# Block 1 of a fused two-matmul kernel with one plain h pair in place of three, and three w1 form stores placed behind the x transposes

## The chip, the cores and the metric

The kernel runs on one core of one Trainium2 chip. The metric is the device time of one execution in microseconds (us), given as the median of several runs. All times inside an execution come from a hardware profile of one run, counted from the start of its span.

## The reference

```python
y = np.matmul(x, w1) + b1                          # x (16, 512, 768), w1 (768, 3072)
y = 0.5 * y * (1.0 + erf(y / np.sqrt(2.0)))        # GELU
return np.matmul(y, w2).astype(np.float32)         # w2 (3072, 768)
```

There are 8192 rows of x. Inputs and output are float32; the kernel computes in bf16 with float32 sums.

## The kernel before

**Row blocks.** The 8192 rows are cut into ten blocks of 768 rows and a last one of 512 (`pairs`; "block p" below is the p-th of them). Each block is computed in two stages: first the hidden layer, whose GELU values go to the tile `g`, then the product with w2, whose sums go through PSUM to the tile `ot` and from there to the output.

**First stage.** The 24 chunks of 128 hidden columns are taken as 12 "h pairs" j = (j, j + 12). There are two ways to compute one h pair for a block.
- Plain: `plain` (matmuls at L396) does 6 matmuls for each of the two columns and each half of the rows, 24 matmuls of 128x384 in all, straight from the bf16 copy of w1.
- Formed: a Winograd scheme of 7 products, P1 to P7 (`product1`, matmuls at L154), 3 matmuls each, 21 in all. It needs 7 "forms" of the w1 pair (sums and differences, made once by `make_w1`: one copy on ScalarE, four sums on VectorE, the halves of which are called `one` and `two`) and four sums of x (`sum_x`, tile `xft`). ScalarE copies P1's bank (`ps<-ps`, L102) before P2 can add to the copy.

In block 0 all pairs are plain. In block 1 the pairs 0, 1 and 2 are plain and nine are formed. In all later blocks twelve are formed. The loop over formed pairs runs in steps: step s works on the pair `js[s]`, and `fill(s)` puts one piece of other work (a half of a form or a sum for the second stage) behind P2 and one behind P6.

**Where forms live.** A set of forms is made in a staging area that is free just then: parts of `ot` (called otf), of `st` (stf), of `ev`, of `xft`. The tuple `order1` says which pair is formed n-th and `stage` where. From the staging area it is stored to DRAM (`w1f`). The stores of n = 0 to 3 are held in the list `waiting`; those of n = 4 and 5 go on SyncE's queue, later ones on GpSimd's. The forms come back from `w1f` through a ring of five slots, which take the place of the raw w1 in `w1t`; a slot can be filled once every raw pair under it has been formed (and, if plain, used): `free_slots`, `fill_slot`. In block 1 the pairs 9 and 10 are read directly from their staging areas instead (`where`).

**Second stage.** A block's rows form two groups, G0 and G1, of three row tiles. A group takes 15 products M0 to M14 (`rest`, `part2`, 8 matmuls each at L229) in the order M14, M8, M4, M7, M6, M13, M12, M2, M1, M5, M3, M10, M9, M11, M0. Most of them read a sum of `g` blocks that VectorE makes (`gsum`: M2a, M2b and so on) in slots of `st`; G1's M2, M12 and M10 have the slots 4, 5 and 6. `finish2` takes each product out of its PSUM bank, with copies on ScalarE and adds on VectorE into `ot`. Several products share a bank: M11 adds to the bank of M10, and M0 to that of M9, so that M0's matmuls need VectorE's add of M9 to be done.

**What sets the order.** Every instruction is kept in program order on its engine, and each queue of DMAs too. Around the end of block 0's first stage SyncE's queue holds two w1 form stores (n = 0 from `ot`, n = 1 from `st` slots 4 to 6), then six transposes (L287) that bring block 1's x into `xt`, then the stores of n = 2 and 3. The loads of x for these transposes are on GpSimd's queue behind all loads of w1 and w2; the fifth and sixth of them reuse the buffers of the first two and so wait for the first two transposes.

Of the kernel before, what the change touches and what calls it, by code (L numbers as in the profile page):

```python
# [12 lines left out]
P = 128  # L13
# [20 lines left out]
def kernel(  # L34
# [21 lines left out]
    QH = QC // 2  # L56
    SLOT = 7 * KH * P
    RING = 5
    PLAIN = 3
    GRP = 3 * KC * P  # L60
    FIRST = -(-2 * GRP // SLOT)
    HOME = (0, None, 2 * GRP, 4 * GRP)
    pairs = []
    r = 0
# [46 lines left out]
    def sub(dst, a, b):  # L111
        inorder(nc.vector.tensor_tensor(out=dst, in0=a, in1=b, op=ALU.subtract))  # L112

    seq = [3, 9, 10, 4, 5, 6, 7, 8, 11] + [j for _ in pairs[2:] for j in range(HP)]
    where = {}

    def fill_slot(k):
# [8 lines left out]
    formed = set()  # L126

    def index(p, j):
        return seq.index(j) if p == 1 else (p - 1) * HP - PLAIN + j

    def place_h(hc):
        h, j = divmod(hc, HP)
# [87 lines left out]
    def gsums(G, *ms):  # L220
        return [lambda m=m: gsum(G, m) for m in ms]
# [8 lines left out]
                out=ps[:, :NB], lhsT=lhs[:, c, :], rhs=w2t[:, c, WF[m], :],  # L230
                start=(m in OPENS and c == 0), stop=(c == QC - 1), skip_group_check=True))

    spare = 1
    turn = {2: 3, 1: 0, 3: 2}

    def store(t, r, last, c0=0, c1=N):
        dma(nc.sync if last else nc.gpsimd, out=of[r:r + P, c0:c1], in_=t[:, c0:c1])
# [100 lines left out]
    def raw(j):  # L338
# [1 line left out]
        return w1_pair(j // 3).rearrange("p (b kc c) -> p b kc c", b=4, kc=KH)[:, :, :, c0:c0 + P]  # L340

    made = 0
    stage = ((otf, 0), (stf, 4 * QC * P), (evf, 0), (xftf, 0), (evf, 0), (xftf, 0),
             (otf, N * 4), (stf, 4 * QC * P), (otf, 0), (stf, QC * P), (stf, 4 * QC * P), (stf, QC * P))
    order1 = (3, 4, 5, 6, 7, 8, 9, 11, 10, 0, 1, 2)
    waiting = []

    def make_w1():
        nonlocal made
        n = made  # L350
        made += 1
        j = order1[n]
        a = raw(j)
        area, o = stage[n]
        s = area[:, o:o + SLOT].rearrange("p (f kc c) -> p f kc c", f=7, kc=KH)
        copy("act", s[:, 0:2], a[:, 1:3])

        def one():
            add(s[:, 2], a[:, 1], a[:, 2])
            add(s[:, 3:5], a[:, 0:4:2], a[:, 1:4:2])  # L360

        def two():
            sub(s[:, 5], a[:, 2], a[:, 0])
            sub(s[:, 6], a[:, 1], a[:, 3])
            if n < 4:
                waiting.append(lambda queue: dma(queue, out=w1f[j], in_=area[:, o:o + SLOT]))
            else:
                dma(nc.sync if n < 6 else nc.gpsimd, out=w1f[j], in_=area[:, o:o + SLOT])
            formed.add(j)
            if j in (9, 10):  # L370
                where[seq.index(j)] = area[:, o:o + SLOT]

        return one, two

    ready = [(k + FIRST) % RING for k in range(RING)]

    def free_slots(plain_done=0):
        while ready:
            k = ready[0]
            need = {j for j in range(HP) if HOME[j // 3] is not None  # L380
                    and HOME[j // 3] < (k + 1) * SLOT and HOME[j // 3] + 2 * GRP > k * SLOT}
            if not need <= formed or any(plain_done <= j < PLAIN for j in need):
                break
            fill_slot(ready.pop(0))

    def form_w1(plain_done=0):
        for f in make_w1():
            f()
        free_slots(plain_done)

    def plain(hc, half):
        py = bank()
# [138 lines left out]
    make_w2(7)  # L531
    for m in ("M1", "M3b", "M10a", "M10b", "M11a", "M11b"):
        gsum(blk[0], m)
    for f in waiting[:2]:
        f(nc.sync)


    ts = [[dict() for _ in range(HP)] for _ in pairs]

    def ahead(p):  # L540
        j = PLAIN if p == 1 else 0
        for m in ("P1", "P7"):
            product1(ts[p][j], m, p, j, pairs[p][1])

    def run(fs):
        for f in fs:
            f()
# [13 lines left out]
    for p, (r0, w) in enumerate(pairs):  # L561
# [3 lines left out]
        full = len(G1["tiles"]) == 3  # L565

        if p > 0:
            js = seq[:HP - PLAIN] if p == 1 else list(range(HP))
            last = len(js) - 1
            more = []  # L570
            if p == 1:
                hcs = [hc for j in range(PLAIN) for hc in (j, HP + j)]
                for n, hc in enumerate(hcs):
                    if n in (0, 1, 3):
                        form_w1()
                    if n in (1, 2):
                        sum_x(2 * n - 2, w)
                        sum_x(2 * n - 1, w)
                    plain(hc, 0)
                    if n == len(hcs) - 1:  # L580
                        ahead(p)
                    plain(hc, 1)
                free_slots(PLAIN)
                more = [0, 1, 3]

            both = (G0, G1) if full else (G0,)
            todo = [(js.index(QH - 1) if QH - 1 in js else 0, f) for G in both for f in gsums(G, *EARLY)]
            todo += [(js.index(2 * QH - 1), f) for G in both for f in gsums(G, *MIDDLE)]
            if p == 1:
                todo[2:4] = [(3, f) for _, f in todo[2:4]]  # L590

            halves = []

            def fill(s):
                if s in more and not halves:
                    more.remove(s)
                    halves.extend(make_w1())
                    halves.append(None)
                if halves and halves[0] is None:
                    halves.clear()  # L600
                elif halves:
                    halves.pop(0)()
                    if len(halves) == 1:
                        halves.clear()
                        free_slots(PLAIN)
                    return
                if s <= last and todo and s > todo[0][0] + (p > 1 or todo[0][0] > 0):
                    todo.pop(0)[1]()

            def step1(s, m):  # L610
                if 0 <= s <= last:
                    product1(ts[p][js[s]], m, p, js[s], w)

            for s in range(last + 1):
                if s == 0:
                    order = ((0, "P2"), (0, "P4"), (-1, "P1"), (0, "P6"))
                elif s == 1:
                    order = ((0, "P7"), (1, "P5"), (0, "P2"), (1, "P3"), (0, "P4"), (0, "P6"))
                else:
                    order = ((0, "P1"), (0, "P7"), (1, "P5"), (0, "P2"), (1, "P3"), (0, "P4"), (0, "P6"))  # L620
                for d, m in order:
                    step1(s - d, m)
                    if m in ("P2", "P6"):
                        fill(s)
            step1(last, "P5")
            part2(G0, "M14", range(0, 5))
            step1(last, "P3")
            part2(G0, "M14", range(5, QC))
            finish2(G0, "M14")
            if nxt is not None:  # L630
                prepare_x(*nxt, otf[:, 2 * G1["o"][2] * K:])
            rest(G0, "M8")
            rest(G0, "M4")
            run([f for _, f in todo] + gsums(G0, *LATE))
            rest(G0, "M7")
            qs = [h * QH + q for q in range(QH) for h in range(2)]
            part2(G0, "M6", qs)
            finish2(G0, "M6")
            part2(G0, "M13", qs)
            finish2(G0, "M13")  # L640
        else:
            raws = ("M4", "M14", "M13", "M8", "M7", "M6")
            prepare_x(*nxt, xftf[:, SLOT:])
            for f in waiting[2:]:
                f(nc.sync)
            for c in range(QC - 1):
                for m in raws:
                    part2(G0, m, (c,))
            for m in raws:
                part2(G0, m, (QC - 1,))  # L650
                finish2(G0, m)
# [10 lines left out]

        if full:
            run(take(9))
            for m in ("M14", "M8", "M4"):
                rest(G1, m)
            if p > 0:
                for k in range(4):
                    sum_x(k, nxt[1])
            for m in ("M7", "M6", "M13"):  # L670
                rest(G1, m)
            if p == 0:
                form_w1()
            middle(G1, lambda n: [form_w1] if p == 0 and n == 5 else [])
            if p > 0:
                ahead(p + 1)
            rest(G1, "M0")
        else:
            a = lambda k: block(G1, 0, k)
            d12, d13 = st[:, 4, :, :], st[:, 5, :, :]  # L680
            sub(d12, a(0), a(1))
            sub(d13, a(0), a(2))
            t = ot[:, G1["o"][2], :]
            for n, terms in enumerate(((("b31", a(2)), ("M4", a(1)), ("b11", d12)),
                                       (("M13", a(2)), ("b22", a(1)), ("b12", d13)))):
                ps = bank()
                for f, lhs in terms:
                    for c in range(QC):
                        inorder(nc.tensor.matmul(  # L689
                            out=ps[:, :NB], lhsT=lhs[:, c, :], rhs=w2t[:, c, WF[f], :],  # L690
                            start=(f == terms[0][0] and c == 0), stop=(f == terms[2][0] and c == QC - 1)))
                copy("act", t[:, n * NB:(n + 1) * NB], ps[:, :NB])
                store(t, G1["rows"][0], True, n * NB, (n + 1) * NB)
# [30 lines left out]
```

## Time and profile before

| what | value |
|---|---|
| median of 3 runs | 881.35 us (881.0 to 882.9) |
| profiled execution | 881.5 us, its span 879.7 us |
| TensorE matmul busy | 872.2 us, 99% of the span |
| VectorE busy | 588.4 us, 67% |
| ScalarE busy | 399.2 us, 45% |
| granted TensorE clock | 1.0 throughout |

The profiled execution takes 1.8 us more than its span, and is 0.15 us above the median. "Busy" is the time in which an engine has an instruction under way. "PE" is TensorE's matmul unit, "DVE" VectorE, "ACT" ScalarE, "POOL" GpSimd, "SP" SyncE; a "q" behind a name is that engine's queue of issued DMAs. "Landing" is the time from a DMA's issue to its completion. Block 0's first stage ends at 57.2 us, its second at 97.6 us, and block 1's first stage at about 140 us.

### The profile page before, as it was taken

To read this page: it belongs to the slowest core of one execution; us is meant where nothing else is said; L and a number is where in the kernel's file an instruction comes from. 1 tells how busy PE (TensorE), PEld (TensorE's weight loads), DVE (VectorE), ACT (ScalarE), POOL (GpSimd) and SP (SyncE) were. 2 spreads that over 40 slices of the span, in tenths; PEclk is the share of its full clock that TensorE was granted. 3 is DMA by queue.
4 is the path that set the end of the run, shared out by engine and by line. 5 is a ranking of instruction groups with operands and counts; after the bars stand their busy time and mean duration, and the time that the engine had idled before them with its cause. 6 is when DMAs were issued, how large, how long until landed. Compare 5 with 4: busy or idle time off the path is not lost.

```text
span 879.7 us, 14114 instructions
## 1 busy us (share of the span) xinstructions
PE 872.2 (99%) x5508; PEld 533.3 (61%) x5508; DVE 588.4 (67%) x1104; ACT 399.2 (45%) x789; POOL 84.4 (10%) x153
## 2 busy tenths in 40 slices
PE   9999999999999999999999999999999999999998
PEld 6665656666666666666666666666666666666774
DVE  2889777757765766677578566756765776577654
ACT  3642384157227613741671276147316712751560
POOL 6200110010110011000101100010001011000000
PEclk9999999999999999999999999999999999999999
DMA  9996589276717734671766277356718663761621
GB/s 195 237 198 162 210 285 276 72 201 202 167 77 225 217 98 126 219 194 64 211 210 163 63 232 210 91 162 211 167 73 225 199 150 84 228 191 54 208 68 72
DMA packets 89031, 147.31 MB, mean 167 GB/s; under 512 B 50796, under 2 KB 68228, under 8 KB 88964
## 3 DMA queue, kind: packets, MB, share of 16 engines
q1 hardware_dynamic: 64832, 97.04, 36.5%
q0 software_dynamic: 24096, 49.36, 23.9%
q8 instruction: 43, 0.70, 0.3%
q14 instruction: 24, 0.20, 0.1%
q10 hardware_dynamic: 36, 0.01, 0.0%
HBM read 123.19 MB, written 33.42 MB: 178 GB/s over the span
## 4 chain that ended last, share of the span: by engine, by line
PE 89%; DMA 6%; DVE 3%; issue 1%; ACT 1%; POOL 0%; DVEq 0%; ACTq 0%; POOLq 0%
PE ps L229 45%; PE ps L154 43%; DMA w2t<-in_w_dram 5%; DVE w2t L112 1%; PE ps L689 1%; DMA w1t<-in_w_dram 1%; ACT g L143 1%; DVE ot L109 0%; DVE st L112 0%; DVE g L112 0%; DVE ps L112 0%; ACT ot L102 0%; DVE st L109 0%; DVE w2t L109 0%; POOL xft L79 0%
## 5 line engine op out<-in xcount | busy, mean ns | idle before, releaser
L154 PEld LDWEIGHTS <-w1t 128*128 128x128 bf16 x2415 | 236.1, 98 | 145.6 <-issue 1.9
L143 ACT ACTIVATE g<-ps,b1t 128x384 bf16<-128x384 f32 (+1 forms) x411 | 222.8, 571 | 78.8 <-PE ps L154 56.2
L154 PE MATMUL ps<-xft,w1t 128*128 128x384 bf16 (+1 forms) x1380 | 257.4, 320 | 0.5 <-ACT ps L102 0.5
L229 PE MATMUL ps<-w2t,g 128*128 128x384 bf16 x1512 | 257.5, 326 | 0.1
L229 PEld LDWEIGHTS <-g 128*128 128x128 bf16 x1512 | 147.9, 98 | 97.7 <-issue 0.3
L154 PE MATMUL ps<-xt,w1t 128*128 128x384 bf16 (+1 forms) x1035 | 201.1, 320 | 0.2
L109 DVE TENSOR_TENSOR ot<-ot,ps 128x384 f32<-128x384 f32 x231 | 125.4, 552 | 108.7 <-PE ps L229 53.1
L229 PE MATMUL ps<-w2t,st 128*128 128x384 bf16 x1008 | 170.8, 326 | 1.0 <-DVE st L109 1.0
L102 ACT COPY ot<-ps 128x384 f32<-128x384 f32 x128 | 60.9, 481 | 232.5 <-PE ps L229 213.9
L229 PEld LDWEIGHTS <-st 128*128 128x128 bf16 x1008 | 98.5, 98 | 66.4 <-DVE st L109 1.4
L102 ACT COPY ps<-ps 128x384 f32<-128x384 f32 (+1 forms) x117 | 53.0, 453 | 134.6 <-PE ps L154 134.6
L112 DVE TENSOR_TENSOR ev<-ps,ev 128x384 f32<-128x384 f32 (+1 forms) x117 | 63.6, 544 | 71.4 <-PE ps L154 70.5
L112 DVE TENSOR_TENSOR ps<-ps,ev 128x384 f32<-128x384 f32 (+1 forms) x117 | 64.6, 552 | 44.4 <-PE ps L154 43.8
L104 DVE COPY ev<-ps 128x384 f32<-128x384 f32 (+1 forms) x117 | 63.3, 541 | 23.1 <-PE ps L154 23.0
L143 ACT ACTIVATE g<-ev,b1t 128x384 bf16<-128x384 f32 (+1 forms) x117 | 70.9, 606 | 11.3 <-DVE ev L112 11.3
L112 DVE TENSOR_TENSOR st<-g 128x1024 bf16<-128x1024 bf16 x107 | 72.9, 682 | 0.9 <-ACT g L143 0.9
L79 POOL DMA_DIRECT2D out_dram<-ot x60 | 32.6, 544 | 343.1 <-DVE ot L109 343.1
L112 DVE TENSOR_TENSOR g<-g 128x1024 bf16<-128x1024 bf16 x84 | 57.4, 684 | 0.4
L79 POOL DMA_DIRECT2D xb<-in_x_dram x38 | 20.6, 548 | 339.7 <-DMA xt<-xb 328.7
L396 PE MATMUL ps<-xt,w1t 128*128 128x384 bf16 x252 | 41.6, 326 | 0.0
L396 PEld LDWEIGHTS <-w1t 128*128 128x128 bf16 x252 | 24.6, 98 | 16.2
L109 DVE TENSOR_TENSOR g<-g 128x1024 bf16<-128x1024 bf16 x42 | 29.0, 689 | 1.1
(70 smaller groups left out, 262.4 us busy)
## 6 DMA issues: line engine op xcount, KB each, us to landing
w1t<-w1f SPq DMA_DIRECT2D x115, 672.0 KB, 4.5
out_dram<-ot POOLq DMA_DIRECT2D x60, 384.0 KB, 2.6
xb<-in_x_dram POOLq DMA_DIRECT2D x38, 192.0 KB, 4.6
w2t<-in_w_dram POOLq DMA_DIRECT2D x8, 576.0 KB, 25.9
ot<-in_x_dram POOLq DMA_DIRECT2D x18, 192.0 KB, 7.8
w1f<-st POOLq DMA_DIRECT2D x4, 672.0 KB, 6.6
w1t<-in_w_dram POOLq DMA_DIRECT2D x4, 576.0 KB, 25.4
w1f<-ev SPq DMA_DIRECT2D x2, 672.0 KB, 3.6
```

Source lines behind the costliest of these rows:

```text
L79: inorder(queue.dma_start(out=out, in_=in_))
L102: inorder(nc.scalar.copy(out=dst, in_=src))
L104: inorder(nc.vector.tensor_copy(out=dst, in_=src))
L109: inorder(nc.vector.tensor_tensor(out=dst, in0=a, in1=b, op=ALU.add))
L112: inorder(nc.vector.tensor_tensor(out=dst, in0=a, in1=b, op=ALU.subtract))
L143: inorder(nc.scalar.activation(out=g[:, place_h(hc), half, :w], in_=src, func=ACTF.Gelu, bias=b1t[:, hc:hc + 1], scale=sign))
L154: inorder(nc.tensor.matmul(out=ps[:, :w], lhsT=forms[:, W1F[m], kc, :], rhs=moving1(m, kc, w), start=(kc == 0 and m in ("P1", "P7")), stop ...
L229: inorder(nc.tensor.matmul(out=ps[:, :NB], lhsT=lhs[:, c, :], rhs=w2t[:, c, WF[m], :], start=(m in OPENS and c == 0), stop=(c == QC - 1), ...
L396: inorder(nc.tensor.matmul(out=py[:, :HW], lhsT=lhs[:, kc, (j % 3) * P:(j % 3 + 1) * P], rhs=xt[:, kc, half, :], start=(kc == 0), stop=(kc ...
L689: inorder(nc.tensor.matmul(out=ps[:, :NB], lhsT=lhs[:, c, :], rhs=w2t[:, c, WF[f], :], start=(f == terms[0][0] and c == 0), stop=(f == ter ...
```

## The change

- Block 1 has one plain pair, 9, instead of three. Eleven pairs are formed. Pairs 6, 7 and 8 are read directly from staging areas.
- The forms are made in another order, and the first six of them before block 1: n = 4 before G1's products in block 0, n = 5 after M13 of G1. The last six are made in block 1, two beside its plain products and four in the steps 0, 2, 3 and 4.
- The four sums of x for block 1 move from beside block 1's plain products to the end of block 0, between VectorE's adds of G1's M10, M9, M11 and M0.
- Of the four held w1 form stores, the first (n = 0) is issued from ScalarE's queue after block 0's plain products; those of n = 1, 2 and 3 go to SyncE's queue behind the transposes. Before, n = 0 and 1 were issued in front of the transposes at about 30 us.
- The ring starts with slot 0. The sums for the second stage of block 1 move to later steps, as the pairs come in another order, and G0's late sums go ahead of G1's.

```diff
-    PLAIN = 3
+    PLAIN = (9,)
+    DIRECT = (6, 7, 8)
...
-    seq = [3, 9, 10, 4, 5, 6, 7, 8, 11] + [j for _ in pairs[2:] for j in range(HP)]
+    seq = [0, 6, 7, 8, 1, 2, 3, 4, 5, 10, 11] + [j for _ in pairs[2:] for j in range(HP)]
...
-    spare = 1
-    turn = {2: 3, 1: 0, 3: 2}
+    spare = 3
+    turn = {2: 1, 1: 0, 3: 2}
...
-    stage = ((otf, 0), (stf, 4 * QC * P), (evf, 0), (xftf, 0), (evf, 0), (xftf, 0),
-             (otf, N * 4), (stf, 4 * QC * P), (otf, 0), (stf, QC * P), (stf, 4 * QC * P), (stf, QC * P))
-    order1 = (3, 4, 5, 6, 7, 8, 9, 11, 10, 0, 1, 2)
+    ST1, ST4, OTB = (stf, QC * P), (stf, 4 * QC * P), (otf, N * 4)
+    stage = ((otf, 0), ST4, (evf, 0), (xftf, 0), (evf, 0), (xftf, 0), ST4, (otf, 0), OTB, ST1, ST4, (otf, 0))
+    order1 = (3, 4, 5, 0, 1, 2, 6, 7, 8, 10, 11, 9)
...
-            if j in (9, 10):
+            if j in DIRECT:
                 where[seq.index(j)] = area[:, o:o + SLOT]
...
-    ready = [(k + FIRST) % RING for k in range(RING)]
+    ready = list(range(RING))
...
-    for f in waiting[:2]:
-        f(nc.sync)
+    waiting.pop(0)(nc.scalar)
...
             if p == 1:
-                hcs = [hc for j in range(PLAIN) for hc in (j, HP + j)]
+                hcs = [hc for j in PLAIN for hc in (j, HP + j)]
                 for n, hc in enumerate(hcs):
-                    if n in (0, 1, 3):
-                        form_w1()
-                    if n in (1, 2):
-                        sum_x(2 * n - 2, w)
-                        sum_x(2 * n - 1, w)
+                    form_w1()
                     plain(hc, 0)
...
-                free_slots(PLAIN)
-                more = [0, 1, 3]
+                more = [0, 2, 3, 4]
...
-            todo = [(js.index(QH - 1) if QH - 1 in js else 0, f) for G in both for f in gsums(G, *EARLY)]
-            todo += [(js.index(2 * QH - 1), f) for G in both for f in gsums(G, *MIDDLE)]
-            if p == 1:
-                todo[2:4] = [(3, f) for _, f in todo[2:4]]
+            done = [max(n for n, j in enumerate(js) if j < k * QH) for k in (1, 2)]
+            todo = [(done[0], f) for G in both for f in gsums(G, *EARLY)]
+            todo += [(done[1], f) for G in both for f in gsums(G, *MIDDLE)]
...
-                if s <= last and todo and s > todo[0][0] + (p > 1 or todo[0][0] > 0):
+                if s <= last and todo and s > todo[0][0] + 1:
                     todo.pop(0)[1]()
...
-            run([f for _, f in todo] + gsums(G0, *LATE))
+            left = [f for _, f in todo]
+            if p == 1:
+                run(left[:-len(MIDDLE)] + gsums(G0, *LATE) + left[-len(MIDDLE):])
+            else:
+                run(left + gsums(G0, *LATE))
...
             prepare_x(*nxt, xftf[:, SLOT:])
-            for f in waiting[2:]:
+            for f in waiting:
                 f(nc.sync)
...
         if full:
             run(take(9))
+            if p == 0:
+                form_w1()
             for m in ("M14", "M8", "M4"):
                 rest(G1, m)
...
             if p == 0:
                 form_w1()
-            middle(G1, lambda n: [form_w1] if p == 0 and n == 5 else [])
+            at = {5: (0,), 6: (1,), 7: (2,)} if p == 0 else {}
+            middle(G1, lambda n: [lambda k=k: sum_x(k, nxt[1]) for k in at.get(n, ())])
             if p > 0:
                 ahead(p + 1)
             rest(G1, "M0")
+            if p == 0:
+                sum_x(3, nxt[1])
```

## The prediction

> **What bounds the kernel now.** I read the page's engine row first: TensorE is busy for 99% of the span, so only fewer matmuls or less idle TensorE can count.
>
> ```profile
> PE 872.2 (99%) x5508; PEld 533.3 (61%) x5508; DVE 588.4 (67%) x1104; ACT 399.2 (45%) x789; POOL 84.4 (10%) x153
> ...
> L396 PE MATMUL ps<-xt,w1t 128*128 128x384 bf16 x252 | 41.6, 326 | 0.0
> ```
>
> The timeline of TensorE comes next (start, duration, instructions). In long runs a 128x384 matmul starts every 0.1625 us: the 66 plain ones from 97.64 to 108.36 us are 10.72 us. Held against this pace, the rows show where TensorE starts late.
>
> ```profile
> 65.03 4.06 PE L229 MATMUL ps<-w2t,st 128*128 128x384 bf16 x24
> 70.10 1.47 PE L229 MATMUL ps<-w2t,st 128*128 128x384 bf16 x8 [1.00 <-DVE st L109]
> ...
> 72.71 2.76 PE L229 MATMUL ps<-w2t,st 128*128 128x384 bf16 x16
> 75.54 10.56 PE L229 MATMUL ps<-w2t,g 128*128 128x384 bf16 x64
> ...
> 109.34 1.14 PE L396 MATMUL ps<-xt,w1t 128*128 128x384 bf16 x6
> 110.99 0.65 PE L154 MATMUL ps<-xft,w1t 128*128 128x384 bf16 x3 [0.51 <-ACT ps L102]
> ```
>
> M5 of block 0's G0 could start at 65.03 + 24 x 0.1625 = 68.93 and starts at 70.10: 1.17 us lost. M11 could start at 72.71 + 16 x 0.1625 = 75.31 and starts at 75.54: 0.23. P2 of block 1's first formed pair could start at 109.34 + 0.975 = 110.32 and starts at 110.99: 0.67. One more of 0.19 us is at 124.41, where the row before gives 123.73 + 3 x 0.1625 = 124.22.
>
> Why M5 is late: the chain of waits is VectorE without a gap from a load of w2 that lands at 53.76 to M5's sum (69.36 in the timeline of VectorE, last fence). The loads are late because the DMA engines are full: their share is over 1.1 in every stretch of 2 us from 4 to 64 us. The DMA view, asked for single loads, gives their landings. They were issued at 13.39, 14.84, 16.31 and 39.83 us.
>
> ```profile
> w2t<-in_w_dram POOLq DMA_DIRECT2D x1, 576.0 KB, 19.8
> ...
> w1t<-in_w_dram POOLq DMA_DIRECT2D x1, 576.0 KB, 24.7
> ...
> w2t<-in_w_dram POOLq DMA_DIRECT2D x1, 576.0 KB, 26.0
> ...
> xb<-in_x_dram POOLq DMA_DIRECT2D x1, 192.0 KB, 20.5
> ```
>
> They land at 33.2, 39.5, 42.3 and 60.3. Loads of this size land 2.85 us apart elsewhere (42.3 to 59.4 in six steps), so the gap of 6.35 holds 3.5 us of other traffic: the two form stores in SyncE's timeline at 29.51 and 30.30.
>
> ```profile
> 29.51 0.33 SPq L79 DMA_DIRECT2D w1f<-ot  x1
> 30.30 0.33 SPq L79 DMA_DIRECT2D w1f<-st  x1
> 60.39 2.63 SPq L287 DMA_TRANSPOSE xt<-xb  x2
> ...
> 68.63 4.03 SPq L287 DMA_TRANSPOSE xt<-xb  x2
> 72.76 0.52 SPq L79 DMA_DIRECT2D w1f<-ev  x1
> ```
>
> **The change part by part.**
>
> Matmuls: pairs 1 and 2 (by count, two of the three plain) go from 24 to 21 matmuls each. 6 x 0.1625 = 0.98 us less. All twelve forms are made before as after, so ScalarE's and VectorE's forms, stores and gathers are only moved. The 8 GELUs of 0.57 us for two pairs stay; a formed pair adds a copy (0.45) on ScalarE and three operations (0.55 each) on VectorE, beside matmuls, as in the other formed steps.
>
> Stores n = 0 and 1 leave 30 us: every load that lands from 39.5 on comes 3.5 us sooner. VectorE's last make_w2 then ends at about 60.7 in place of 64.2, and its next six sums (3.9 us) at 64.6, before the first of block 0's products is to be added (65.0). M5's sum is then ruled by M12's add (matmuls done at 66.33): 66.5 + 0.5, and the sum to 67.7, before 68.93. The 1.17 goes, and the 0.23 too, as M10's add follows its matmuls at once: 1.40 us.
>
> Store n = 0 now stands on ScalarE's queue behind the last GELU (58.02) and in front of M4's copy (64.42). ScalarE is idle for these 6.4 us, so its issue (0.33 on SyncE's row, 0.54 on GpSimd's) is covered. M14's copy and M7's add write over its source and wait for its landing: 3.3 us (the `ev` store at 72.76) to 7.7 (the `st` store among loads), so 61.7 to 66.1. I take 63.5, as the loads end at 60 us. At 66.1 M14's copy ends at 66.5, 0.2 after M2 wants its bank, and M5's sum at 68.6, still in time. Cost 0, at worst 0.2.
>
> Store n = 1 now stands behind the transposes. It reads `st` slots 4 to 6, and G1's M2a writes slot 4. M2a therefore waits for its landing. Queued behind M2a on VectorE is M9's add, and TensorE's M0 waits for that.
>
> ```profile
> 69.36 0.68 DVE L109 TENSOR_TENSOR st<-g 128x1024 bf16<-128x1024 bf16 x1
> ...
> 75.41 0.68 DVE L112 TENSOR_TENSOR st<-g 128x1024 bf16<-128x1024 bf16 x1
> 76.01 0.54 DVE L109 TENSOR_TENSOR ot<-ot,ps 128x384 f32<-128x384 f32 x1
> ```
>
> The third row is M9's add, 0.60 behind M2a. After the change M0 is due at 68.93 + 5 x 1.30 = 75.43, so M2a must start by 75.43 - 0.05 - 0.54 - 0.60 = 74.25. The transposes: the first waits for its load (60.3, now 56.8) and for block 0's plain matmuls (57.4), so starts at 57.45, 2.9 sooner. Its landing (3.7 us) lets the fifth load go, and so on as before: SyncE is through at 72.7 - 2.9 = 69.8, n = 1 goes first and lands 3.3 us later, at 73.1. VectorE reaches M2a at 73.45. No wait; 1.1 us are to spare.
>
> n = 2 and 3 land some 2 us after n = 1 (75 to 77); the next use of `ev` is at about 81. n = 4's form (1.35 us) in front of G1's products, and n = 5's at 85.8, lie where VectorE waited 0.70 and 0.75 for ScalarE anyway. The four sums of x (0.66 each) between the adds: M10's add ends at 94.5 on the old clock, the sum at 95.2, M9's add at 95.7, M0 due at 96.34; 0.6 to spare. `xft` is free at 91.2 (n = 5's store, 87.4 + 3.8).
>
> Block 1's start: n = 8 is the first form there whose area waits for G1's last output store. Before, forms from 103.06 on waited for such a store (5.6 us landing, among fills), and ScalarE, working off that backlog, copied P1 late: the 0.67. After, the store lands in 2.6 to 5.6 us, at about 100 to 103; VectorE needs the area at 102.3, ScalarE its half, which the store before frees 1.1 sooner, at 101.7; and P1's copy stands in front of both. The 0.67 goes. The 0.19 came from a form's ScalarE copy waiting 0.60 for a store from the same `st` area, one step after it; now four steps lie between: it goes too. Steps 2, 3 and 4 each carry a form; in a step of 3.41 us ScalarE then has 2.4 (its rows from 120.09 on) + 0.74, VectorE 1.7 (three of 0.55) + 1.4: both fit.
>
> Ring: the last form (step 4) frees slots 3 and 4, and pair 4 is needed at step 7, 5.6 us after that fill can go. Before, the fill at 124.1 had the same 5.6 us (step 6 at 129.77) with the same store and x loads behind it, and landed in 4.4. No cost. The sums for `st` move to steps 8 to 10 and behind them; as many (11) as before stand between the last step and M7's add.
>
> Sum: 0.98 + 1.40 + 0.67 + 0.19 = 3.24 us. The profiled 881.5 becomes 878.3 (it was 0.15 above the median, which I leave).
>
> **The rivals.**
>
> 1. The moved store slows the transposes. n = 0 moves at 59 to 63 us beside them; if they lose what the loads lost to one store (3.5 / 2 = 1.75), n = 1 lands at 74.85, M0 0.6 late: 878.9. For it: the DMA share was over 1.1 there. Against: 3.5 us of other traffic has left the stretch. The Trainium skill, "DMA: Bandwidth & Descriptors", section "Issuing engines are not separate DMA queues", says that DMAs of ScalarE, SyncE and GpSimd run on the same 16 engines and interleave; by it the store is not free on a queue of its own. The gap of 6.35 us agrees.
>
> 2. The loads do not come sooner (another limit than bandwidth). The 1.40 stays, n = 1 lands at 72.76 + 3.3 = 76.1, M9's add ends 1.2 later, and M0 moves from 76.84 to 77.3: 881.5 - 0.98 - 0.86 + 0.46 = 880.1. Against: the gap stands exactly where the stores are.
>
> 3. Pair 4's fill is late. At the landing of the next fill before (9.0 us at 125.5) step 7 waits 3.4: 881.7, no change. For: forms in steps 3 and 4 put two stores closer to the fill. Against: 4.4 in the same place.
>
> 4. Slower: n = 1's landing. VectorE stands at M2a until then, with M9's add and M0 behind. From 77.5 on the loss eats the 3.24; from 79.2 the kernel is slower by over 0.2%. With the transposes as before and that store's own landing of before (7.7), it lands at 80.5, M0 starts at 81.7, 6.3 late: 884.5. For: it was placed behind six transposes. Against: the 3.3 of the store that stood there.
>
> 5. The change does less in block 1: ScalarE's backlog stays (0.67 and 0.19), 879.1.
>
> **How the numbers follow.** Forecast 0.50; rival 1 0.17, 2 0.08, 3 0.10, 4 0.10, 5 0.05. A difference under 0.2% (1.76 us) can't be told from none. Forecast, 1 and 5 are below 879.6: faster 0.72. 2 and 3 are within: 0.18. 4: slower 0.10. The range takes the forecast and rivals 1, 2 and 5 (0.80): from 877.5 (0.4 for the medians' spread and 0.4 for small idle times not listed) to 881.0 (880.1 with the spread of before's runs).
>
> **What would show it.** 5502 matmuls; no late start at block 0's M5, M11 and M0, nor at block 1's first P2; the first transpose at 57.5 and w2's loads 3.5 us sooner; M2a of G1 at 73.5 to 74.3. An idle TensorE at M0 with VectorE waiting for `w1f<-st` would show rivals 1, 2 or 4 by its size; an idle TensorE at the start of step 7 of block 1, waiting for `w1t<-w1f`, rival 3.

## The result and the profile after

| what | before | after |
|---|---|---|
| median, same chip (5 runs each) | 881.35 us (881.0 to 883.31) | 878.16 us (877.83 to 878.35) |
| profiled execution, its span | 881.5 us, 879.7 us | 877.96 us, 876.2 us |
| TensorE matmuls, busy | 5508, 872.2 us | 5502, 870.6 us |

The ratio is 0.9956, with a 95% interval of 0.9945 to 0.9967: faster by 3.2 us. Of the 3.5 us between the two spans, 0.19 lies ahead of everything that was changed: block 0's second stage starts at 57.04 instead of 57.23, as TensorE's first plain matmul ran that much earlier. From there to the end it is 819.16 us instead of 822.47: 3.31 us, where the prediction's sum was 3.24.

The first line is the engine row of the page after, the second the group of plain matmuls, 204 in place of 252.

```profile
PE 870.6 (99%) x5502; PEld 532.9 (61%) x5502; DVE 591.8 (68%) x1110; ACT 400.4 (46%) x791; POOL 84.4 (10%) x153
...
L396 PE MATMUL ps<-xt,w1t 128*128 128x384 bf16 x204 | 33.8, 326 | 0.0
```

The timeline of TensorE after (start, duration, instructions) answers to the rows with late starts. None of these rows has a wait any more.

```profile
64.84 5.36 PE L229 MATMUL ps<-w2t,st 128*128 128x384 bf16 x32
70.04 1.46 PE L229 MATMUL ps<-w2t,g 128*128 128x384 bf16 x8
71.34 2.76 PE L229 MATMUL ps<-w2t,st 128*128 128x384 bf16 x16
73.94 10.56 PE L229 MATMUL ps<-w2t,g 128*128 128x384 bf16 x64
...
99.94 1.14 PE L396 MATMUL ps<-xt,w1t 128*128 128x384 bf16 x6
100.92 0.65 PE L154 MATMUL ps<-xft,w1t 128*128 128x384 bf16 x3
```

The 24 matmuls ahead of M5 and M5's 8 are now one row of 32; M11 starts at 73.94 = 71.34 + 16 x 0.1625, M0 is inside the row of 64, and P2 of block 1's first formed pair starts at 100.92 = 99.94 + 0.975. The row at 124.39 follows the one at 123.90 after 3 x 0.1625. All four gaps are closed.

The same four loads in the DMA view, one by one. They were issued at 12.65, 14.11, 15.57 and 35.93 us.

```profile
w2t<-in_w_dram POOLq DMA_DIRECT2D x1, 576.0 KB, 20.1
...
w1t<-in_w_dram POOLq DMA_DIRECT2D x1, 576.0 KB, 21.5
...
w2t<-in_w_dram POOLq DMA_DIRECT2D x1, 576.0 KB, 22.9
...
xb<-in_x_dram POOLq DMA_DIRECT2D x1, 192.0 KB, 20.6
```

They land at 32.75, 35.6, 38.5 and 56.5. The gap between the first two, 6.35 us before, is 2.86, like the one behind it.

What had been left thin is seen on SyncE's queue and on VectorE:

```profile
56.61 3.62 SPq L287 DMA_TRANSPOSE xt<-xb  x2
60.34 2.81 SPq L287 DMA_TRANSPOSE xt<-xft  x2
67.00 2.78 SPq L287 DMA_TRANSPOSE xt<-xb  x2
69.97 0.43 SPq L79 DMA_DIRECT2D w1f<-st  x1
```

```profile
66.27 1.48 DVE L109 TENSOR_TENSOR ot<-ot,ps 128x384 f32<-128x384 f32 x3 [2.04 <-ACT ot L102]
67.67 0.68 DVE L109 TENSOR_TENSOR st<-g 128x1024 bf16<-128x1024 bf16 x1
...
73.72 0.68 DVE L112 TENSOR_TENSOR st<-g 128x1024 bf16<-128x1024 bf16 x1
74.32 0.54 DVE L109 TENSOR_TENSOR ot<-ot,ps 128x384 f32<-128x384 f32 x1
```

M5's sum runs from 67.67 to 68.35 and is due at 64.84 + 24 x 0.1625 = 68.74. Store n = 1 is issued at 69.97 and lands 3.3 us later, at 73.3. M2a (73.72) does not wait. M0 is due at 73.94 + 8 x 0.1625 = 75.24, so by the prediction's steps M2a must start by 75.24 - 0.05 - 0.54 - 0.60 = 74.05: the store has 0.75 us to spare, VectorE 0.3.

### The profile page after: what moved, and what is told of

Read it like the earlier page. It is cut to its first block, busy times and chain, and to the rows that moved or that the text cites. A ratio compares the mean times of both kernels' runs of the same rounds, so it can differ in the third digit from the quotient of the medians.

```text
span 876.2 us, 14116 instructions
## 1 busy us (share of the span) xinstructions
PE 870.6 (99%) x5502; PEld 532.9 (61%) x5502; DVE 591.8 (68%) x1110; ACT 400.4 (46%) x791; POOL 84.4 (10%) x153
## 4 chain that ended last, share of the span: by engine, by line
PE 98%; DVE 1%; ACT 0%; issue 0%; DVEq 0%; ACTq 0%
PE ps L229 47%; PE ps L154 44%; PE ps L396 5%; PE ps L691 1%; PE ps L459 1%; PE ps L406 1%; PE ps L421 0%; DVE ps L112 0%; DVE st L112 0%; DVE ev L112 0%; ACT g L143 0%; DVE ev L104 0%; DVE g L112 0%; DVE xt L104 0%; ACT ot L102 0%
## 5 line engine op out<-in xcount | busy, mean ns | idle before, releaser
L154 PEld LDWEIGHTS <-w1t 128*128 128x128 bf16 x2436 | 238.2, 98 | 146.1 <-issue 0.9
L396 PE MATMUL ps<-xt,w1t 128*128 128x384 bf16 x204 | 33.8, 326 | 0.0
L109 DVE TENSOR_TENSOR st<-st,g 128x1024 bf16<-128x1024 bf16 x42 | 28.9, 688 | 0.8
```

The lines of the kernel that those rows point to most:

```text
L154: inorder(nc.tensor.matmul(out=ps[:, :w], lhsT=forms[:, W1F[m], kc, :], rhs=moving1(m, kc, w), start=(kc == 0 and m in ("P1", "P7")), stop ...
L396: inorder(nc.tensor.matmul(out=py[:, :HW], lhsT=lhs[:, kc, (j % 3) * P:(j % 3 + 1) * P], rhs=xt[:, kc, half, :], start=(kc == 0), stop=(kc ...
```

## The experiments

All kernels are the changed one with one edit, but for the second, which is the kernel before with one edit. Each has its median, range and number of runs; on the chips used, the kernel before measured 882.12 us (for the first four experiments), 882.19 (the next two) and 882.22 (the last three), and the ratios are against these. To compare profiles, I use the time from the start of block 0's second stage to the end of the span: before 822.47, after 819.16.

**Stores n = 0 and 1 back at 30 us.**

```diff
-    waiting.pop(0)(nc.scalar)
+    for f in waiting[:2]:
+        f(nc.sync)
...
-            for f in waiting:
+            for f in waiting[2:]:
```

> The changed kernel with the first two form stores (n = 0 and 1) issued in front of the transposes as before; all of block 1's part is kept. Theory (the stores at 30 us delay the w2 and x loads by 3.5 us): the load after the stores lands 6.35 us after the one ahead of it, block 0's M5 is late by 1.17 us and M11 by 0.23 again, the first transpose starts near 60.4, and the span is 1.40 longer than the changed kernel's 876.2: 877.6 (time 879.4). Rival (the gain in block 0 comes from something else in the change, such as the order of forms): M5 on time, span 876.2.

Measured: 880.34 us (879.58 to 881.18, 11 runs), 0.9978 of before [0.9970, 0.9987]. From the stage's start to the end 820.98, 1.82 more than the changed kernel. TensorE's timeline:

```profile
64.92 4.06 PE L229 MATMUL ps<-w2t,st 128*128 128x384 bf16 x24
70.41 1.48 PE L229 MATMUL ps<-w2t,st 128*128 128x384 bf16 x8 [1.43 <-DVE st L109]
```

M5 was due at 68.82 and is 1.59 late, M11 0.23 late: 1.82, all of the difference, at the two places named, while block 1's gaps stay closed. The amount is above the 1.40 because the loads landed 0.29 later and the stage began 0.11 earlier than in the profile of before. The stores among the loads cause M5's late start: shown.

**The move of the stores alone, in the kernel before.**

```diff
-    for f in waiting[:2]:
-        f(nc.sync)
+    waiting.pop(0)(nc.scalar)
...
-            for f in waiting[2:]:
+            for f in waiting:
```

> The kernel before with only the move of the form stores (n = 0 on ScalarE's queue, n = 1 to 3 behind the transposes). Theory: M5 and M11 of block 0 on time, 1.40 us less, while block 1's late P2 (0.67) and the 0.19 stay: span 879.7 - 1.4 = 878.3, time 880.1. M2a of G1 starts at 73.7 and does not hold up M0. Rival (the store in front of M2a costs what it saves when the rest of the change is not there): M0 late, span 879.7 or more.

Measured: 880.38 us (880.0 to 882.34, 11 runs), 0.9984 [0.9975, 0.9992]. Eight executions took 880.0 to 880.9, three 881.9 to 882.3. The profile caught one of the three (881.92). In it M5 and M11 are on time, but M0 is not. TensorE and VectorE:

```profile
74.60 1.46 PE L229 MATMUL ps<-w2t,g 128*128 128x384 bf16 x8
77.55 9.26 PE L229 MATMUL ps<-w2t,g 128*128 128x384 bf16 x56 [1.49 <-DVE ot L109]
```

```profile
76.34 0.69 DVE L112 TENSOR_TENSOR st<-g 128x1024 bf16<-128x1024 bf16 x1 [1.88 <-DMA w1f<-st]
76.95 0.55 DVE L109 TENSOR_TENSOR ot<-ot,ps 128x384 f32<-128x384 f32 x1
```

The second row of the VectorE fence is M9's add, held behind M2a, which waits for store n = 1. M0 was due at 74.60 + 1.30 = 75.90: 1.65 late. The chain behind it is the DMA view's landing of the first transpose:

```profile
xt<-xb SPq DMA_TRANSPOSE x1, 7.3
```

It was issued at 57.60, so the fifth load went at 65.47, the transpose of it at 70.25, n = 1 at 72.98, and that landed 3.3 us later. So M5 and M11 are on time with the stores moved, and what I had put down as "1.1 us to spare" is used up in some executions: the rival came true in this one. That the eight shorter executions have M0 on time is likely, but none of them was profiled.

Block 1 is the old one here, so the 0.67 and the 0.19 should have stayed. P2 of the first formed pair, due at 111.02, starts at 111.55: 0.53 late. The row of six at 124.78 follows that of three at 124.30 without a gap: the 0.19 is gone although the order and the areas of the forms are those of before.

**Only n = 0 back in front.** It is issued from SyncE at 30 us; n = 1 stays behind the transposes.

```diff
-    waiting.pop(0)(nc.scalar)
+    waiting.pop(0)(nc.sync)
```

> The changed kernel with store n = 0 alone issued on SyncE's queue in front of the transposes (at about 29 us); n = 1 to 3 stay behind them. Theory: the loads lose 1.75 us, half of 3.5, which the 2.04 us that VectorE waits before M7's add in the changed kernel cover; nothing moves beside the transposes, so the first of them lands in 3.7 us and not 5.8, which makes up for its later start. M5 on time, span 876.2, so the queue of ScalarE buys nothing by itself. Rival (all 3.5 us of relief are needed): M5 late by 0.6 or more, span 876.8 or more.

Measured: 879.11 us (878.49 to 879.19, 5 runs), 0.9960 [0.9946, 0.9973]; from the stage's start 820.23, 1.07 more than the changed kernel.

```profile
64.97 4.06 PE L229 MATMUL ps<-w2t,st 128*128 128x384 bf16 x24
69.43 1.47 PE L229 MATMUL ps<-w2t,st 128*128 128x384 bf16 x8 [0.39 <-DVE st L109]
```

One store among the loads costs them 1.7 us, half of the 3.5: GpSimd, which issues the loads, waits 3.85 us for the landing that it delays, in place of 2.17. I had expected M5 to be on time even so; in this profile it is 0.56 late, M11 0.22 and M0 about 0.30. The reason is on VectorE. The load of w2 from which it works on without a gap landed 3.1 us later than in the profile of the changed kernel (first row; the second row is this run):

```profile
49.93 0.63 DVE L109 TENSOR_TENSOR w2t<-w2t 128x384 bf16<-128x384 bf16 x2 [1.01 <-DMA w2t<-in_w_dram]
...
53.07 0.63 DVE L109 TENSOR_TENSOR w2t<-w2t 128x384 bf16<-128x384 bf16 x2 [1.95 <-DMA w2t<-in_w_dram]
```

The store explains 1.7 us of that. The rest is not the store's: in a second profile of the changed kernel (below) the same load landed at 51.61, and VectorE's wait before M7's add was 0.76 us and not the 2.04 that I had counted on. So the expectation failed in the profile: the 2.04 us of cover were read from one execution, and others have less. In the times nothing is shown: the profiled execution is the slowest of the five, and 3.0 us less than before in the median can't be told from the changed kernel's 3.2. The first transpose landed in 3.7 us here, with no store beside it.

**Store n = 1 as the third of its queue instead of the first.**

```diff
-            for f in waiting:
+            for f in waiting[1:] + waiting[:1]:
```

> The changed kernel with store n = 1 behind those of n = 2 and 3 instead of in front of them. Theory (VectorE stands at M2a until n = 1 has landed, M9's add behind it, TensorE's M0 behind that): n = 1 is issued at about 71 and lands 5.6 us later, as the third store does now, at 76.6; M9's add ends at 77.75, M0 starts at 77.8 in place of 75.24, 2.56 late: span 878.8, time 880.5. Rival (M0 has slack, or the bank is free in another way): no lateness, span 876.2.

Measured: 883.18 us (881.02 to 884.72, 11 runs), 1.0006 [0.9997, 1.0015]; 882.2 us of span in the profile, 5.33 more than the changed kernel from the stage's start. VectorE, TensorE, and TensorE's clock by stretch (columns: us, its length, then busy time of PE, PEld, DVE, ACT and POOL, granted clock, DMA share, GB/s):

```profile
78.36 0.69 DVE L112 TENSOR_TENSOR st<-g 128x1024 bf16<-128x1024 bf16 x1 [3.89 <-DMA w1f<-st]
```

```profile
74.61 1.47 PE L229 MATMUL ps<-w2t,g 128*128 128x384 bf16 x8
79.57 10.94 PE L229 MATMUL ps<-w2t,g 128*128 128x384 bf16 x56 [3.49 <-DVE ot L109]
```

```profile
79.00:80.00 1.00, 0.43 (x3) 0.29 (x3) 1.00 (x3) 0.00 (x0) 0.00 (x0) 1.00 0.00 0
80.00:81.00 1.00, 1.00 (x6) 0.54 (x4) 1.00 (x3) 0.00 (x0) 0.12 (x1) 0.61 0.00 0
81.00:82.00 1.00, 1.00 (x5) 0.46 (x4) 0.46 (x2) 0.00 (x0) 0.43 (x1) 0.50 0.00 0
...
84.00:86.00 2.00, 2.00 (x15) 1.21 (x13) 1.97 (x4) 0.96 (x2) 0.00 (x0) 1.00 0.31 123
```

Behind two more stores n = 1 landed in 5.6 us instead of 3.3, and the first transpose took 5.3: M0, due at 75.91, is 3.66 late (2.56 was expected). Then comes what I had not expected at all: the clock falls to 0.50 and M0's row of 56 takes 10.78 us to its next start in place of 56 x 0.1625 = 9.10. That is 1.68 more, and 3.66 + 1.68 = 5.34 is the whole difference. The three fastest executions (881.0 to 881.6) had a mean granted clock of 1.0, the eight others (882.6 to 884.7) of 0.996 to 0.998. So the place of rival 4 is real. The change stays clear of this loss by the order of three stores on one queue.

**Store n = 0 behind the transposes too**, in front of n = 1.

```diff
-    waiting.pop(0)(nc.scalar)
```

> The changed kernel with all four held stores behind the transposes on SyncE's queue, n = 0 first. It tells two things. If the store on ScalarE's queue is what made the first transpose land in 5.8 us (3.7 before), it lands in about 3.7 here and SyncE is through with the transposes some 2 us sooner, near 67.9; if not, 5.8 stays and SyncE is through at 69.9. Then n = 0 lands 3.3 us after it, at 71.2 or 73.3, and ScalarE's copy of M14 and VectorE's M7 add wait for that in place of going at 64.6: M2, due at 66.14, and M5 behind VectorE's sums start late by 5 to 8 us, span 881 to 884. Rival (ScalarE's copies have that much slack): span 876.2.

Measured: 886.87 us (886.63 to 888.09, 4 runs), 1.0062 [1.0047, 1.0077]: slower than before. TensorE and ScalarE:

```profile
65.53 1.46 PE L229 MATMUL ps<-w2t,st 128*128 128x384 bf16 x8
73.66 6.67 PE L229 MATMUL ps<-w2t,st 128*128 128x384 bf16 x24 [6.66 <-ACT ot L102]
```

```profile
73.12 2.01 ACT L102 COPY ot<-ps 128x384 f32<-128x384 f32 x5 [7.72 <-DMA w1f<-ot]
```

M14's copy writes over n = 0's source and waits for its landing; M2, due at 66.83, starts 6.83 late (5 to 8 was expected). Here too the clock is at 0.50 after the gap: 24 matmuls take 6.51 us in place of 3.90, another 2.61, which no expectation had. The first transpose, issued at 58.58 with no store beside it, landed in

```profile
xt<-xb SPq DMA_TRANSPOSE x1, 3.7
```

In the experiment before, with n = 0 beside it, it was issued at 58.56 and landed in 5.3. So the store on ScalarE's queue does lengthen the transpose, by 1.6 us between these two.

**Block 1's staging areas.** Three of the late forms change their areas: n = 6 and n = 10 go to `OTB`, n = 8 to `ST4`. Of these, only n = 6 then has the area that it had in the kernel before.

```diff
-    stage = (..., ST4, (otf, 0), OTB, ST1, ST4, (otf, 0))
+    stage = (..., OTB, (otf, 0), ST4, ST1, OTB, (otf, 0))
```

> The changed kernel with the areas of forms n = 6 and n = 8 exchanged (and that of n = 10 with them), so that the first form of block 1 waits for G1's last output stores and not the third. Theory (ScalarE, held by a form that waits for an output store, copies P1 late, and P2 waits): ScalarE's copy for n = 6 moves from 86.8 to 98.8, where M11's output store lands, P1's copy ends near 102.5, and block 1's first P2, due at 100.92, starts 1.6 late: span 877.8, time 879.6. Rival (that 0.67 of before came from the amount of work on ScalarE, not from the wait): P2 late by under 0.3, span 876.2 to 876.5.

Measured: 880.19 us (879.97 to 882.44, 10 runs), 0.9981 [0.9972, 0.9991]; 1.51 more than the changed kernel from the stage's start. ScalarE, then TensorE:

```profile
99.63 0.83 ACT L102 COPY ot<-w1t 128x768 bf16<-128x768 bf16 x1 [13.18 <-issue]
...
102.50 0.50 ACT L102 COPY ps<-ps 128x384 f32<-128x384 f32 x1
```

```profile
100.63 1.14 PE L396 MATMUL ps<-xt,w1t 128*128 128x384 bf16 x6
103.05 0.65 PE L154 MATMUL ps<-xft,w1t 128*128 128x384 bf16 x3 [1.28 <-ACT ps L102]
```

The form's copy waits for an output store from its area. The row shows "issue", but M11's output store was issued at 96.48 and landed in 3.1 us, at 99.6, just before the copy starts. ScalarE's queue backs up, P1's copy is late and P2 starts 1.44 late (1.6 expected). The theory held: which area the first form of block 1 uses decides over that gap.

**The changed kernel again, and two ways to make the spare time larger.** The first of the two takes the sum M2a one place later, behind M9's add, so that the add no longer stands behind it; the second issues n = 1 from ScalarE behind n = 0.

```diff
-        middle(G0, lambda n: take(1) if n >= 5 else [])
+        middle(G0, lambda n: take(1) if n >= (6 if p == 0 else 5) else [])
...
-            run(take(9))
+            run(take(10))
```

```diff
-    waiting.pop(0)(nc.scalar)
+    for f in (waiting.pop(0), waiting.pop(0)):
+        f(nc.scalar)
```

> The changed kernel itself, beside the next two on one chip, and for how its single executions spread. Theory (store n = 0 on ScalarE's queue makes the first transpose land in 5.3 to 7.3 us; where it is near 7.3, n = 1 lands after 74.3 and M0 is late): about 3.2 us less than before in most executions, 1.5 to 2.3 above that in about one of six. Rival (the late M0 of the kernel with the stores alone belongs to that kernel only): no upper group.

> The changed kernel with G1's M2a (and M3a and M12 with it) one place later on VectorE: behind M9's add, not in front of it. Theory (M9's add is what M0 waits for, and M2a only stands in front of it): where n = 1 lands in time nothing changes, the span is that of the changed kernel within 0.2 us; where it lands late, M0 is on time and the wait falls on M11's add, which TensorE needs 2.6 us later: no execution more than 1 us above the fastest. Rival (VectorE has no room behind M0's add): every execution longer by 0.6 us, the length of one sum.

> The changed kernel with both stores n = 0 and n = 1 on ScalarE's queue behind block 0's last GELU; only n = 2 and 3 stay behind the transposes. Theory: n = 1 lands at about 66, well before M2a (73.7), so M0 can't be late by it; the transposes lose another 1.75 us to it, the first lands in about 7.5 us and SyncE is through with them near 72; the store of n = 2 then lands at about 76 to 78, still before ScalarE needs that area (78.0). Span as the changed kernel's, no upper group. Rival (the transposes end so late that the form n = 4, in front of M14's copy on ScalarE, waits for n = 2's store): G1's M14 and the products on its bank late by 1 to 2 us, span 877 to 878.

Measured: the changed kernel 878.95 us (878.06 to 881.07, 7 runs; 0.9968 [0.9956, 0.9979]), M2a later 878.66 (877.79 to 878.75, 5 runs; 0.9958 [0.9946, 0.9970]), n = 1 on ScalarE 878.52 (877.39 to 878.64, 5 runs; 0.9956 [0.9945, 0.9968]). The changed kernel's profile, of an execution of 878.37, shows VectorE on the edge:

```profile
74.44 0.69 DVE L112 TENSOR_TENSOR st<-g 128x1024 bf16<-128x1024 bf16 x1 [0.24 <-DMA w1f<-st]
75.05 0.55 DVE L109 TENSOR_TENSOR ot<-ot,ps 128x384 f32<-128x384 f32 x1
```

M9's add ends at 75.60 and M0 is due at 75.65. The first transpose had landed in 5.3 us, n = 1 was issued at 71.10. Four of its seven executions, 878.95 to 881.07, are above everything that the two other kernels gave; in the first measurement all five had been between 877.8 and 878.4. I had expected one execution in six to be 1.5 to 2.3 us above the others; here four in seven are, by 0.8 to 3.0 us. With M2a later, the VectorE rows are

```profile
73.97 0.56 DVE L109 TENSOR_TENSOR ot<-ot,ps 128x384 f32<-128x384 f32 x1 [0.34 <-PE ps L229]
75.49 0.69 DVE L112 TENSOR_TENSOR st<-g 128x1024 bf16<-128x1024 bf16 x1 [0.96 <-DMA w1f<-st]
```

M9's add goes first, M2a waits 0.96 for a store that came as late as in the profile of the second experiment (the first transpose took 7.7 us), and TensorE runs 64 matmuls in one row from 73.77: M0 loses nothing. With n = 1 on ScalarE, M0 is on time as well. In the median the three can't be told apart (their intervals overlap); what the two edits take away is the upper part of the spread, in five runs each. Five runs are few for that: the changed kernel's first five had no upper part either. That the changed kernel's long executions have a late M0 follows from the profiled one of the second experiment and from the 0.05 us above; none of them was profiled itself.

## Where the prediction held, and the step that failed

**Sign and size came true.** The sum was 3.24 us and the profile gives 3.31; 878.3 was forecast and 878.16 measured. The gaps that were to close did close, those at M5, M11 and P2 for the reason written. What was to cover the moved stores was wrong in two steps, and there the number held by luck. The terms, one by one:

- Matmuls, 0.98: six fewer are counted (5502). No run isolates this term. The kernel with the stores put back is 1.78 under before in the medians (880.34 against 882.12), where this term and the two of block 1 were 1.84 together.
- M5 and M11, 1.40: closed; undone, 1.82 at the same two places. The size was that of one profile and moves by some tenths with the landing of the loads.
- The first P2, 0.67: closed. The areas decide over it, as written; with the first form of block 1 behind M11's output store it came out at 1.44, and in the second experiment, with the old block 1, at 0.53.
- The 0.19 at 124.41: closed in the profile, but it was closed in the second experiment too, whose block 1 is that of before. So this gap comes and goes without the change, and the account of it (four steps between two forms) is not shown.
- Covered at no cost, and so found: pair 4's fill was issued at 117.54 and landed in 4.4 us, 1 us ahead of its step; M11's and M0's output stores landed in 3.0 and 3.2; the sums of x between the adds cost nothing; store n = 0 landed in 4.9 us, at 62.2 (63.5 was written), ahead of M14's copy.

**The step that failed is the one on the transposes**: "the first waits for its load (60.3, now 56.8) and for block 0's plain matmuls (57.4), so starts at 57.45", its "landing (3.7 us)", "and so on as before", "No wait; 1.1 us are to spare." It started at 56.61 in the profile after, right behind its load (56.5) and before all plain matmuls were done, so only those of its own half of the rows hold it. And it landed in 5.8 us, not 3.7; in the other profiles with n = 0 beside it in 5.3 to 7.8, and in 3.7 in all three kernels where that store was elsewhere (and before). The two errors nearly cancel in this profile (69.97 for the store in place of 69.8), so the forecast number held by luck, but the store has 0.75 us to spare there and not 1.1, hardly any in the second profile of the same kernel (M2a at 74.44 for 75.65 - 1.19 = 74.46), and was 1.6 late in the profile of the stores' move alone. I had this mechanism as rival 1, at 1.75 us, with a late M0 at 0.6 and 878.9. The mechanism is real, and its size was at the low end (5.8 - 3.7 = 2.1 in the profile, 1.6 to 4.0 elsewhere with that one store); I held it for unlikely as "3.5 us of other traffic has left the stretch". But the traffic that left was at 30 us, and the store stood in the stretch itself. So it was not a rival to the forecast: the longer landing is in every profile with the store there, and a late M0 comes of it in some executions and not in others.

**M7's add**, the second step that failed, was put at 65.0 and began at 66.27: it waited 2.04 us for ScalarE, whose copy out of the same bank ended then. M5's sum was written to be over at 67.7, "ruled by M12's add"; it only started at 67.67, behind the adds of M7, M6 and M12 in one row, and ended at 68.35. So 0.39 us were to spare to M5 and not the 1.2 of the prediction. The change got through with that; with n = 0 in front and the loads late, M5 and M11 lost 0.78.

**The rivals.** 2 (loads not sooner) fell: the gap closed from 6.35 to 2.86. 3 (the fill) and 5 (ScalarE's backlog) did not occur in the profile. 4 was the right place and the wrong price: with n = 1 third in its queue M0 was 3.66 late, and the loss was 5.34 with the clock's part; my 884.5 for a delay of 6.3 us had no such part, and the run in which a product was 6.83 late lost another 2.61.

## What to carry to other kernels

When a store is moved away from loads that are late, look for the transfer that it now stands beside, and price that transfer at no less than what the loads lost to the store, not at its old landing; a chain of four DMAs with about 1 us to spare is not covered. Put the instruction that waits for such a store behind those that others wait for (M9's add ahead of M2a): here that cost nothing, and the lateness of the store then cost nothing either. Take the spare time of a step from more than one profile: VectorE's wait before M7's add was 2.04 us in one execution of the changed kernel and 0.76 in another. And hold a gap in TensorE's work for dearer than its length once it is as long as the two below.

## What the runs showed of the hardware that I had not expected

**The clock after a gap.** Gaps of up to 1.49 us left the granted clock at 1.00. After 3.49 us idle it fell to 0.50 for some 3.4 us, from 0.6 us after the matmuls had started again (1.68 us lost); in the gap of 6.66 us it fell while TensorE was still idle, and stayed at 0.50 until 79 us (2.61 lost in 24 matmuls). The Trainium skill, "TensorE: Matmul & The Clock Gate", section "What's actually happening", says that the throttled state is the default and comes back after an idle window of about 3.4 us, at half the pulses. Both of these runs agree, with 0.50 and with the 3.49 that was enough; how long a gap the three executions without the loss had is open, as none of them was profiled.

**A transpose beside a store.** The first x transpose of 3.7 us took 5.3 to 7.7 with one store of 672 KB beside it, on another engine's queue, and 7.8 with two; the figure changed between executions of one kernel (5.8 and 5.3 for the changed one). The Trainium skill, "DMA: Bandwidth & Descriptors", section "Issuing engines are not separate DMA queues", has the rule: transfers from different engines interleave on the same 16 DMA engines. The runs agree. Why it is 5.3 in one execution and 7.7 in another stays open. The time of issue alone doesn't decide it: issued at 57.60 in two kernels, 0.3 us before the store in both, it landed in 5.3 in one and 7.3 in the other.
